# Encoder trunk in split float32r: sequence 1's last steps of the second MLP product, moved from the loop to behind it

## The chip, the cores and the metric

The kernel runs on one core of a Trainium2 chip. A core has five engines that run their own instruction streams in order and wait for each other on semaphores: TensorE (PE in the profile) multiplies matrices into PSUM, VectorE (DVE) and ScalarE (ACT) work elementwise on SBUF and PSUM, GpSimd (POOL) elementwise on SBUF, and SyncE (SP) issues most of the DMAs. The metric is the device time of one execution in microseconds. Before the change it is 1680.16 us, the median of three runs (1679.12 to 1681.12).

## The reference

Two sequences of 512 tokens with 1024 features go through two layers and a last norm. Layer 0 mixes tokens with a 2-D Fourier transform, layer 1 with grouped-query attention; each is followed by a squared-ReLU MLP.

```python
def sq_relu_mlp(h, w_up, w_down):
    a = jnp.maximum(h @ w_up, 0)
    return (a * a) @ w_down

for i in range(DEPTH):
    j = i // N_MIXERS
    if i % N_MIXERS == 0:
        x = x + fourier_mix(rms_norm(x, fourier_norm[j]), fourier_w_out[j])
    else:
        x = x + gqa_attention(rms_norm(x, attn_norm[j]), attn_w_qkv[j], attn_q_norm[j],
                              attn_k_norm[j], attn_w_o[j])
    x = x + sq_relu_mlp(rms_norm(x, mlp_norm[i]), mlp_w_up[i], mlp_w_down[i])
return rms_norm(x, final_norm)
```

## The kernel before, in words

**Number format.** All large products run in float32r, each operand split into a high and a low half, three matmuls for one product. A split is a ScalarE copy (L86) and a VectorE subtraction (L87). A split with a gain per feature is a ScalarE activation (L90) and a VectorE instruction (L91); `make_h` uses it for the operands of attention.

**The residual.** Both sequences' residual streams are held transposed, features on partitions: `xs[q, m]` with q = 0, 1 the sequence and m = 0 to 3 a quarter of the features, each tile 128 x 2 x 512. The half of a quarter is called `fo` = 2m or 2m + 1. `put_away` stores such a tile to DRAM (`park`) with a DMA on the SP queue. `square` has ScalarE square one half (L160); GpSimd adds the squares of all eight halves into one tile (L164), and `sums` has TensorE add that tile over the partitions (L172), which gives the sum of squares for each token. `token_scale` turns it into the scale of the RMS norm, in a chain of short VectorE and ScalarE instructions (L135 to L140).

**The MLP.** Both sequences together go through each layer's MLP as a 2 x 2 block product with seven products in place of eight (Winograd's form). The second product, `second_product`, loops over groups of the hidden features and over m. For each m it has two `Row` products and five `Sums` products, whose results VectorE adds from PSUM (L1113) to `xs[0, m]`, `xs[1, m]` or to `e[m]`, a tile that is part of several results. TensorE's order is as written; the other engines' order is set by a scheduler. The weights arrive by DMA (`w_row`, `w_sum`), are combined on VectorE (L1183, L1184, L1190) and split (L86, L87). When all products of an m are done, `finish(m)` adds `e[m]` to a half of `xs[0, m]` (L1253) and to both halves of `xs[1, m]` (L1254), and calls `ready(m)`.

**Between the layers.** In layer 0 `ready(m)` makes, for both sequences and both halves, the operand of attention (`make_h`) and the square, and stores the tile. Behind the loop come the tables for the rotary embedding (16 VectorE instructions, L1382, from a table `rope` and the gains `grow`, both loaded by DMA on SP), and then the products for queries, keys and values. `begun` starts the four token tiles of sequence 0's keys and values with six of eight feature chunks, 72 matmuls; the scale of sequence 0, the remaining 24 matmuls, the scale of sequence 1 and its four tiles of 24 matmuls each follow. VectorE, ScalarE and GpSimd normalize and rotate the keys tile by tile (L1440 is the last step of a tile), and TensorE transposes sequence 0's keys (L1451).

**After layer 1's loop** nothing is made ready: the last two pairs of hidden features, kept apart as plain weights (`w_down`), are projected one eighth of the features at a time, `project(0, fo)` for sequence 0 first (matmuls L81 to L83, the addition L891), each followed by a square and a gain for the output; sequence 1 follows.

Of the kernel before, what the change touches and what calls it, by code (L numbers as in the profile page):

```python
# [19 lines left out]
P = 128  # L20
D = 1024
S = 512
NSEQ = 2
NT = S // P
KC = D // P
# [19 lines left out]
def trunk_kernel(ctx, tc, x_in, xt_in, y_out, tables, rope, gfour, gcol, grow, gfin,  # L45
                 w_four, w_nyq, w_qkv, w_o, w_a22, w_up, w_row2, w_row4, w_sum2, w_sum4, w_down):
    nc = tc.nc
# [13 lines left out]
    def nm(s):  # L61
        n_[0] += 1
        return f"{s}_{n_[0]}"

    def slot(shape, dt):
        return act.tile(shape, dt, tag="u4", name=nm("u"))

    def tm(shape=(P, 512), dt=F32):
        return tmp.tile(list(shape), dt, tag="t2", name=nm("t"))
# [4 lines left out]
    def ps():  # L74
        return psp.tile([P, 512], F32, tag="ps", name=nm("ps"))
# [4 lines left out]
    def mm3(out, lh, ll, rh, rl, first, last):  # L80
        nc.tensor.matmul(out, lh, rh, start=first, stop=False)  # L81
        nc.tensor.matmul(out, lh, rl, start=False, stop=False)  # L82
        nc.tensor.matmul(out, ll, rh, start=False, stop=last)  # L83
# [5 lines left out]
    def split_scaled(dst_hi, dst_lo, src, scale):  # L89
        nc.scalar.activation(dst_hi, src, AF.Copy, scale=scale)  # L90
        nc.vector.scalar_tensor_tensor(dst_lo, src, scale, f32(dst_hi), ALU.mult, ALU.subtract)  # L91
# [34 lines left out]
    def rsqrt(out, ss, n, inv, room=None):  # L126
        for step in rsqrt_steps(out, ss, n, inv, room=room):
            step()
# [16 lines left out]
    xs, acc, apart = {}, {}, {}  # L145
# [6 lines left out]
    def xt(q, fo):  # L152
        return xs[q, fo // 2][:, fo % 2]

    def square(q, fo, n=512, alone=False, first=0):

        if fo == first:
            acc[q] = tm()
        s = acc[q] if fo == first else tm()
        nc.scalar.activation(s[:, :n], xt(q, fo)[:, :n], AF.Square)  # L160
        if alone:
            apart[q] = s
        elif fo != first:
            nc.gpsimd.tensor_add(acc[q][:, :n], acc[q][:, :n], s[:, :n])  # L164

    def sums(q, n=NT):

        o = ps()
        parts = [acc[q]] + ([apart.pop(q)] if q in apart else [])
        for t in range(n):  # L170
            for i, x in enumerate(parts):
                nc.tensor.matmul(o[:, 2 * t : 2 * t + 2], x[:, t * P : (t + 1) * P], ones,  # L172
                                 start=i == 0, stop=i == len(parts) - 1)
        return o[:, 0 : 2 * n : 2], o[:, 64:]
# [9 lines left out]
    def make_h(q, fo, g0):  # L184

        h = slot([P, 2, 512], F32R)
        split_scaled(h[:, 0], h[:, 1], xt(q, fo), gc[:, g0 + fo : g0 + fo + 1])
        return h
# [3 lines left out]
    def put_away(q, i):  # L192
        nc.sync.dma_start(park[q, i], xs[q, i])
# [475 lines left out]
    def even_outs(q, fos):  # L669
        return outs(q, fos, we, 0, 258, (wn.w, un[q]))  # L670
# [30 lines left out]
    ET = mybir.EngineType  # L701
    with tc.manual_schedule(engines={ET.PE, ET.Activation, ET.DVE, ET.Pool, ET.SP}):
# [128 lines left out]
        blocks = Blocks(0)  # L831
# [11 lines left out]
        for fo in range(KC):  # L843
            e, = even_outs(1, [fo])
# [14 lines left out]
        rows = []  # L859
# [234 lines left out]
    def second_product(l, blocks, rows, late=lambda: None, ready=lambda m: None):  # L1094
        e, new = [], [True] * 4
# [154 lines left out]
        def finish(m):  # L1250
            left[m] -= 1
            if left[m] == 0:
                nc.vector.tensor_add(xs[0, m][:, 1], xs[0, m][:, 1], e[m])  # L1253
                nc.vector.tensor_add(xs[1, m], xs[1, m], e[m].unsqueeze(1).broadcast_to([P, 2, 512]))  # L1254
                ready(m)

        first_product(l, blocks, rows, ahead)
# [16 lines left out]
        rows, sums = items[0]  # L1274
# [28 lines left out]
        for k, (rows, sums) in enumerate(items):  # L1303
# [40 lines left out]
            for r in rows:  # L1344
                finish(r.m)
            finish(sums.m)


    hT, rs, wkv = [[], []], [], []

    def token_scale(q):
        r = sm.tile([P, NT], F32, tag="rs", name=nm("rs"), bufs=2)
        ss, room = sums(q)
        rsqrt(r, ss, NT, 1.0 / D, room)
        rs.append(r)
# [4 lines left out]
        wkv.append(lent())  # L1360
        split(*wkv[-1], raw)

    def ready(m):
        for q in range(NSEQ):
            for fo in range(2 * m, 2 * m + 2):
                hT[q].append(make_h(q, fo, KC))
                square(q, fo)
            put_away(q, m)

    second_product(0, blocks, rows, late, ready)  # L1370

    gb = tm((P, 4, HD))
    nc.sync.dma_start(gb, grow.to_broadcast([P, 4, HD]))
# [12 lines left out]
    def qkv(cg, q, t, ws, k0=0, k1=KC, o=None):  # L1386
        o = ps() if o is None else o
        cols = slice(t * P, (t + 1) * P)
        for k in range(k0, k1):
            w = ws[k // 2]  # L1390
            c = (k % 2) * 512
            mm3(o, hT[q][k][:, 0, cols], hT[q][k][:, 1, cols],
                w[0][:, c : c + 512], w[1][:, c : c + 512], k == 0, k == KC - 1)
        return o
# [176 lines left out]
    transposes = {(0, 0, 0): 0, (0, 1, 0): 1}  # L1571

    begun = [qkv(2, 0, t, wkv, 0, KC - 2) for t in range(NT)]
    token_scale(0)
    keeping, turned = keep(), iter(())
    ws = {2: wkv}
# [104 lines left out]
    blocks = Blocks(2 * KC)  # L1681
    nc.scalar.activation(one[:, :1], last[:, :1], AF.Sqrt)

    todo, e, rows = heads_out.plain_sums(), [tm() for _ in range(4)], []
    load_xs(0, park[0])

    def add(x, o):
        nc.vector.tensor_add(x, o, x)
# [9 lines left out]
    with tc.manual_schedule(engines={ET.PE}):  # L1698
# [39 lines left out]
        for j, (m, i) in enumerate(turn()):  # L1738
# [3 lines left out]
            fo = 2 * m + 1 - i  # L1742
# [12 lines left out]
                blocks.first_lo(j - 3)  # L1755
        for i in range(2, 4):
            blocks.first_lo(i)
    second_product(1, blocks, rows)
    ats = []
    for f in range(2 * PLAIN):  # L1760
        raw = load_raw(plain[f], (P, 2, 512))
# [50 lines left out]
    def tokens(t):  # L1812

        x = slot([P, D], F32)
        for h in range(2):
            o = ps()
            for k in range(4):
                nc.tensor.transpose(o[:, k * P : (k + 1) * P], xt(1, 4 * h + k)[:, t * P : (t + 1) * P], ident)
            nc.scalar.copy(x[:, h * 512 : (h + 1) * 512], o)
        return x  # L1820

    with tc.manual_schedule(engines={ET.PE, ET.Activation, ET.DVE, ET.Pool, ET.SP}):
        oa, ob, oc, oe = OutT(0, 4), OutT(1, 2), Out(2), Out(3)
        for fo in range(KC):
            project(0, fo, ws, [a[0] for a in ats])
            square(0, fo)
            oa.gain(fo)
        xtok = [tokens(2), tokens(3)]
        for fo in range(KC):
            project(1, fo, ws, [a[1] for a in ats], 256)  # L1830
            square(1, fo, 256, fo == KC - 1)
            ob.gain(fo)
            if fo == 1:
                oa.root()
            if fo == 3:
                oa.spread()
            if fo > 3:
                oa.write(fo - 4)

        x, z = xtok  # L1840
        y = slot([P, D], F32), slot([P, D], F32)
        groups = ((0, 512), (512, 768), (768, 1024))

        def tile(t, c0, c1, at=0, mid=lambda: None):
            o = ps()[:, : c1 - c0]
            for k in range(len(ats)):
                ak, wk = ats[k][1], ws[k]
                cols = slice(t * P, (t + 1) * P)
                mm3(o, ak[0][:, cols], ak[1][:, cols], wk[0][:, c0:c1], wk[1][:, c0:c1], k == 0, k == len(ats) - 1)
                if k == at:  # L1850
                    mid()
            return o

        def add(x, o, c0, c1):
            nc.vector.tensor_add(x[:, c0:c1], o, x[:, c0:c1])

        def write(x, y, r, i):
            sl = slice(i * 512, i * 512 + 512)
            nc.vector.scalar_tensor_tensor(y[:, sl], x[:, sl], r, gf[:, sl], ALU.mult, ALU.mult)

        o = [tile(2, 0, 512, 2, ob.root)]
        add(x, o[0], 0, 512)
        o.append(tile(2, 512, 1024, 0, ob.spread))
        oc.square(x[:, :512], 0)
        ob.write(0)
        add(x, o[1], 512, 1024)
        oc.square(x[:, 512:], 1)
        o = [tile(3, 0, 512)]
        ob.write(1)
        ob.write(2)  # L1870
        root = oc.root(1)
        for step in root[:2]:
            step()
        ob.write(3)
        for step in root[2:]:
            step()
        add(z, o[0], *groups[0])
        oe.square(z[:, :512], 0)
        write(x, y[0], oc.r, 0)
        o += [tile(3, *g) for g in groups[1:]]  # L1880
        add(z, o[1], *groups[1])
        oe.square(z[:, 512:768], 1)
        write(x, y[0], oc.r, 1)
        nc.sync.dma_start(y_out[2][:P], y[0])
        root = oe.root(2)
        add(z, o[2], *groups[2])
        oe.square(z[:, 768:], 2)
        nc.vector.tensor_mul(y[1][:, 512:768], z[:, 512:768], gf[:, 512:768])
        root[0]()
        root[1]()  # L1890
        nc.vector.tensor_mul(y[1][:, 768:], z[:, 768:], gf[:, 768:])
        for step in root[2:]:
            step()
        nc.scalar.activation(y[1][:, 512:], y[1][:, 512:], AF.Copy, scale=oe.r)
        nc.scalar.dma_start(y_out[2][P:, 512:], y[1][:, 512:])
        write(z, y[1], oe.r, 0)
        nc.sync.dma_start(y_out[2][P:, :512], y[1][:, :512])
# [151 lines left out]
```

## Time and profile before

| | us |
|---|---|
| median of three runs | 1680.16 (1679.12 to 1681.12) |
| the profiled execution's own time | 1682.5 |
| its span, first to last instruction | 1680.5 |
| TensorE busy | 1666.0 |
| VectorE busy | 1258.9 |
| ScalarE busy | 873.4 |
| GpSimd busy | 394.5 |
| layer 0's second product ends, queries, keys and values begin | at 708.6 of the span |
| layer 1's second product ends, the last projections begin | at about 1624 of the span |

The mean granted TensorE clock is 0.998 of full speed.

How to read the rows: a row of the timeline has the start in microseconds, how long the group took, the engine, the line of the code, the operation, what is written and read, and in brackets the engine's idle time before it and who ended it. Equal instructions that follow each other are one row (xN). A row of the windows has the stretch, its length, then for TensorE, its weight loads, VectorE, ScalarE and GpSimd the busy time and the number of instructions, the granted clock, the DMA engines' busy share and GB/s. A row of the waits has who waited for whom, the sum in microseconds, how often, and the longest. A group's row has the count, the busy time, the mean in ns, and the idle time before it. Of a line or a tile, one row gives the shortest, median and longest duration in ns and the first and last start.

### The profile page before, as it was taken

What the parts mean: (1) busy time and instruction counts of PE and PEld (TensorE: products, weight loads), DVE (VectorE), ACT (ScalarE), POOL (GpSimd) and SP (SyncE); (2) the same over time, 40 slices, a digit from 0 to 9 for tenths busy, and PEclk for the clock granted to TensorE, in tenths of its full rate; (3) what the DMA queues carried; (4) which work ended last, traced back from release to release, by engine and by line L of the source; (5) the groups of instructions that cost most, each with busy time, mean ns of one, the idle gap of its engine ahead of it and who ended that gap; (6) DMA issues with size and microseconds to landing.
All of it is one profiled execution on the core that took longest, in us unless ns stands there. A gap on an engine that the chain in (4) does not pass through costs nothing.

```text
span 1680.5 us, 22279 instructions
## 1 busy us (share of the span) xinstructions
PE 1666.0 (99%) x7845; PEld 1387.7 (83%) x7845; DVE 1258.9 (75%) x1848; ACT 873.4 (52%) x1537; POOL 394.5 (23%) x364
## 2 busy tenths in 40 slices
PE   9999999999999999999999999999999999999998
PEld 8988888888888888788878888888888888888887
DVE  8879776557786779869888877777855487878865
ACT  6766444456343425447698854554544553433334
POOL 3321443221000001325544303004422220000002
PEclk9999999999999999999999999999999999999999
DMA  9843655459775757425501146334544696757532
GB/s 310 262 151 111 209 194 182 145 176 371 242 231 170 254 171 225 168 65 196 168 1 39 63 164 224 124 114 160 209 156 155 226 367 203 232 158 237 176 102 100
DMA packets 122047, 302.99 MB, mean 180 GB/s; under 512 B 12200, under 2 KB 13352, under 8 KB 121936
## 3 DMA queue, kind: packets, MB, share of 16 engines
q1 hardware_dynamic: 98576, 254.05, 43.6%
q0 software_dynamic: 8960, 21.05, 5.9%
q10 hardware_dynamic: 14400, 26.48, 4.2%
q8 instruction: 61, 1.00, 0.2%
q14 instruction: 50, 0.41, 0.1%
HBM read 218.11 MB, written 82.38 MB: 179 GB/s over the span
## 4 chain that ended last, share of the span: by engine, by line
PE 87%; DVE 6%; ACT 3%; issue 2%; DMA 2%; POOL 0%; SPq 0%; DVEq 0%; ACTq 0%; POOLq 0%
PE ps L907 69%; PE ps L83 5%; PE ps L81 5%; PE ps L82 5%; PE ps L1482 1%; DVE w L87 1%; ACT t L1474 1%; ACT u L86 1%; DVE u L87 1%; DVE u L219 1%; DVE u L235 1%; DVE u L1113 0%; DMA u<-w_four 0%; DMA u<-x 0%; PE ps L172 0%
## 5 line engine op out<-in xcount | busy, mean ns | idle before, releaser
L907 PE MATMUL ps<-u,w 128*128 128x512 f32 x4944 | 1133.3, 390 | 2.9 <-DVE w L87 2.1
L907 PEld LDWEIGHTS ps<-u,w 128*128 128x128 f32 x4944 | 927.5, 188 | 199.1 <-DVE w L87 3.2
L86 ACT CAST w<-raw 128x1024 fp32r<-128x1024 f32 (+1 forms) x216 | 214.0, 996 | 310.9 <-PE ps L907 229.0
L87 DVE TENSOR_TENSOR w<-raw,w 128x1024 fp32r<-128x1024 f32 (+1 forms) x216 | 252.3, 1172 | 77.6 <-ACT w L86 77.3
L86 ACT CAST u<-u 128x1024 fp32r<-128x1024 f32 x144 | 145.2, 1049 | 83.8 <-PE ps L907 36.5
L87 DVE TENSOR_TENSOR u<-u,u 128x1024 fp32r<-128x1024 f32 x144 | 173.3, 1230 | 19.0 <-ACT u L86 17.9
L907 PE MATMUL ps<-u,u 128*128 128x512 f32 x600 | 143.1, 389 | 0.1
L1142 POOL DMA_DIRECT2D raw<-w_sum x32 | 27.7, 866 | 469.3 <-DMA raw<-w_sum 197.9
L1113 DVE TENSOR_TENSOR u<-ps,u 128x512 f32<-128x512 f32 x160 | 109.6, 686 | 37.2 <-PE ps L907 34.4
L1023 POOL TENSOR_TENSOR u<-u 128x512 f32<-128x512 f32 x28 | 37.7, 1345 | 424.7 <-ACT u L920 424.7
L907 PEld LDWEIGHTS ps<-u,u 128*128 128x128 f32 x600 | 112.5, 188 | 23.8 <-ACT u L938 0.5
L81 PE MATMUL ps<-u,u 128*128 128x512 f32 (+2 forms) x340 | 128.8, 381 | 0.4 <-ACT t L1474 0.3
L82 PE MATMUL ps<-u,u 128*128 128x512 f32 (+2 forms) x340 | 124.2, 366 | 0.4 <-DVE u L87 0.3
L83 PE MATMUL ps<-u,u 128*128 128x512 f32 (+2 forms) x340 | 124.4, 366 | 0.1
L164 POOL TENSOR_TENSOR t<-t,t 128x512 f32<-128x512 f32 (+1 forms) x54 | 77.8, 1446 | 190.6 <-ACT t L160 189.9
L919 ACT ACTIVATE t<-t 128x512 f32<-128x512 f32 x64 | 40.5, 632 | 109.8 <-DVE t L992 99.8
L87 DVE TENSOR_TENSOR u<-ps,u 128x512 fp32r<-128x512 f32 (+3 forms) x112 | 68.5, 635 | 7.9 <-ACT u L86 7.3
L83 PEld LDWEIGHTS ps<-u,u 128*128 128x128 f32 x340 | 64.2, 189 | 10.5 <-DVE u L448 0.5
L81 PEld LDWEIGHTS ps<-u,u 128*128 128x128 f32 x340 | 64.3, 189 | 10.1 <-ACT u L86 1.5
L82 PEld LDWEIGHTS ps<-u,u 128*128 128x128 f32 x340 | 64.4, 189 | 9.2 <-DVE u L87 1.4
L979 DVE TENSOR_TENSOR t<-ps,u 128x512 f32<-128x512 f32 x32 | 22.0, 688 | 60.5 <-PE ps L907 52.7
L1476 POOL TENSOR_SCALAR t<-t,s 128x512 f32<-128x512 f32 x64 | 47.3, 740 | 74.0 <-DVE s L1475 60.1
(260 smaller groups left out, 2029.7 us busy)
## 6 DMA issues: line engine op xcount, KB each, us to landing
raw<-w_up SPq DMA_DIRECT2D x80, 512.0 KB, 4.6
u<-spill_t SPq DMA_DIRECT2D x60, 512.0 KB, 6.8
raw<-w_sum SPq DMA_DIRECT2D x56, 512.0 KB, 5.7
u<-spill_b SPq DMA_DIRECT2D x45, 512.0 KB, 6.2
spill_t<-u SPq DMA_DIRECT2D x84, 256.0 KB, 2.0
spill_b<-t ACTq DMA_DIRECT2D x60, 256.0 KB, 4.3
raw<-w_row SPq DMA_DIRECT2D x28, 512.0 KB, 5.2
park<-u SPq DMA_DIRECT2D x24, 512.0 KB, 4.5
```

What stands on the lines that cost most here:

```text
L81: nc.tensor.matmul(out, lh, rh, start=first, stop=False)
L82: nc.tensor.matmul(out, lh, rl, start=False, stop=False)
L83: nc.tensor.matmul(out, ll, rh, start=False, stop=last)
L86: nc.scalar.copy(dst_hi, src)
L87: eng.tensor_sub(dst_lo, src, f32(dst_hi))
L164: nc.gpsimd.tensor_add(acc[q][:, :n], acc[q][:, :n], s[:, :n])
L907: nc.tensor.matmul(o, w[x][:, sl], h[k][y], start=first and k + i == 0, stop=k == n - 1 and i == 2, skip_group_check=not first)
L919: nc.scalar.activation(t, src, AF.Relu)
L1023: eng.tensor_sub(t[:, 0], b12, b11)
L1113: nc.vector.tensor_add(x, o, x)
L1142: nc.gpsimd.dma_start(s[:, 1], w[:, 3], accum_op=ALU.add)
L1476: nc.gpsimd.tensor_scalar(p, p, sm_[:, :1], 1.0, ALU.mult, ALU.mult)
```

## The change

`finish` no longer adds `e[m]` to sequence 1 and makes only sequence 0 ready. `second_product` returns a function `other(m)` that does the addition to `xs[1, m]`. In layer 0 it is called behind the begun products, for m = 0 to 3, each time followed by sequence 1's squares, operands and store, with VectorE and ScalarE in the written order there. In layer 1 it is called in the loop of sequence 0's projection, for the first four `fo`. `ready` now does the square of a half ahead of its operand. No arithmetic is added or removed.

```diff
@@ second_product
             left[m] -= 1
             if left[m] == 0:
                 nc.vector.tensor_add(xs[0, m][:, 1], xs[0, m][:, 1], e[m])
-                nc.vector.tensor_add(xs[1, m], xs[1, m], e[m].unsqueeze(1).broadcast_to([P, 2, 512]))
                 ready(m)
...
             finish(sums.m)
 
+        def other(m):
+            nc.vector.tensor_add(xs[1, m], xs[1, m], e[m].unsqueeze(1).broadcast_to([P, 2, 512]))
+
+        return other
...
-    def ready(m):
-        for q in range(NSEQ):
-            for fo in range(2 * m, 2 * m + 2):
-                hT[q].append(make_h(q, fo, KC))
-                square(q, fo)
-            put_away(q, m)
-
-    second_product(0, blocks, rows, late, ready)
+    def ready(m, q=0):
+        for fo in range(2 * m, 2 * m + 2):
+            square(q, fo)
+            hT[q].append(make_h(q, fo, KC))
+        put_away(q, m)
+
+    other = second_product(0, blocks, rows, late, ready)
...
     begun = [qkv(2, 0, t, wkv, 0, KC - 2) for t in range(NT)]
+    with tc.manual_schedule(engines={ET.Activation, ET.DVE}):
+        for m in range(4):
+            other(m)
+            ready(m, 1)
     token_scale(0)
...
-    second_product(1, blocks, rows)
+    other = second_product(1, blocks, rows)
...
             project(0, fo, ws, [a[0] for a in ats])
             square(0, fo)
             oa.gain(fo)
+            if fo < 4:
+                other(fo)
```

## The prediction

> **What bounds the kernel now.** I read the page first, then TensorE's waits, then the timeline around the one wait that counts.
>
> ```profile
> span 1680.5 us, 22279 instructions
> PE 1666.0 (99%) x7845; PEld 1387.7 (83%) x7845; DVE 1258.9 (75%) x1848; ACT 873.4 (52%) x1537; POOL 394.5 (23%) x364
> PE ps L907 <- DVE w L87: 2.1, 2, 1.9
> PE ps L907 <- DVE u L1688: 0.7, 1, 0.7
> ```
>
> TensorE is busy 99% of the span, so moving VectorE (DVE), ScalarE (ACT) or GpSimd (POOL) work pays only where TensorE stops. In the products (L907) it stops for L87, the lower half of a weight split, twice, 2.1 us in all, 1.9 of it in one wait. The next rows place that wait and show the clock behind it.
>
> ```profile
> 660.62 12.63 PE L907 MATMUL ps<-u,w 128*128 128x512 f32 x55
> 696.46 12.34 PE L907 MATMUL ps<-u,w 128*128 128x512 f32 x46 [1.91 <-DVE w L87]
> 708.64 0.39 PE L81 MATMUL ps<-u,u 128*128 128x512 f32 x1
> ...
> 698.00:699.00 1.00, 1.00 (x3) 0.74 (x3) 1.00 (x2) 1.00 (x3) 0.40 (x1) 0.50 0.71 262
> 699.00:700.00 1.00, 1.00 (x4) 0.77 (x3) 0.00 (x0) 1.00 (x2) 1.00 (x2) 0.50 1.07 287
> 700.00:701.00 1.00, 1.00 (x4) 0.80 (x3) 0.69 (x1) 0.02 (x1) 1.00 (x1) 0.50 0.79 168
> 701.00:702.00 1.00, 1.00 (x5) 0.80 (x5) 0.00 (x0) 0.00 (x0) 0.92 (x2) 0.96 0.99 397
> ...
> 685.00:694.50 9.50, 9.50 (x43) 7.57 (x41) 9.47 (x10) 5.36 (x8) 7.69 (x4) 1.00 0.36 118
> ```
>
> The wait ends at 696.46, at the end of layer 0's second product. A full-clock matmul takes (12.63-0.39)/54 = 0.227 us. The 46 after the wait take 12.18 us until the next line starts at 708.64, against 46 x 0.227 = 10.43: 1.75 us more, and in those microseconds the granted clock is 0.50. So the wait costs 1.9 + 1.75 = 3.7 us. In the 9.5 us before it VectorE is busy for 9.47: its backlog is the cause.
>
> **The change, part by part: inside the loops.** By the built program's order, the addition L1254 of m = 1 and 2 and sequence 1's L91 of all m leave the crowded stretch (the addition of m = 0 is written behind the loop too, but the scheduler still places it inside). The rows price them.
>
> ```profile
> L1254 DVE TENSOR_TENSOR u<-u,t 128x1024 f32<-128x1024 f32 x3 | 3.7, 1222 | 0.0
> L91 DVE SCALAR_TENSOR_TENSOR u<-u,gc,u 128x512 fp32r<-128x512 f32 x12 | 11.3, 960 | 0.1
> ...
> 667.53 2.98 POOL L164 TENSOR_TENSOR t<-t,t 128x512 f32<-128x512 f32 x2 [0.62 <-ACT t L160]
> 667.98 1.38 DVE L91 SCALAR_TENSOR_TENSOR u<-u,gc,u 128x512 fp32r<-128x512 f32 x1
> 669.28 1.77 DVE L1184 TENSOR_TENSOR raw<-raw 128x512 f32<-128x512 f32 x1
> ```
>
> Five of them stood ahead of the split that TensorE waited for, two L1254 and three L91: 2 x 1.22 + 3 x 0.96 = 5.3 us of VectorE, and GpSimd's additions of sequence 1's squares go with them. The last three rows show what those do: a VectorE instruction with both operands in SBUF (L91, L1184) takes twice its time while GpSimd adds; the two take turns. 5.3 us is well over the wait of 1.9, so I expect it to vanish with the slow clock behind it: **-3.7 us**. Layer 1's loop gains nothing; TensorE has no wait there:
>
> ```profile
> 1410.00:1624.00 214.00, 214.00 (x945) 177.10 (x944) 172.65 (x226) 77.85 (x88) 10.38 (x12) 1.00 0.60 190
> ```
>
> **Behind layer 0's loop.** Here the moved work must be done again in time. What TensorE does there, and the prices:
>
> ```profile
> 724.96 0.95 PE L172 MATMUL ps<-ones,t 128*128 128x2 f32 x8
> ...
> 732.23 0.39 PE L81 MATMUL ps<-u,u 128*128 128x512 f32 x1
> ...
> 754.00 1.03 PE L1451 MATMUL ps<-ident,u 128*128 128x128 f32 x8
> ...
> 712.18 0.69 DVE L1253 TENSOR_TENSOR u<-u,t 128x512 f32<-128x512 f32 x1
> 714.86 3.04 DVE L91 SCALAR_TENSOR_TENSOR u<-u,gc,u 128x512 fp32r<-128x512 f32 x2 [0.38 <-ACT u L90]
> ...
> L1382 DVE SCALAR_TENSOR_TENSOR u<-raw,t x16: 277/278/1154, 718.0 to 722.0; 128x128 f32<-128x128 f32 x16
> ...
> 713.60 0.62 ACT L160 ACTIVATE t<-u 128x512 f32<-128x512 f32 x1
> 714.12 0.70 ACT L90 ACTIVATE u<-u,gc 128x512 fp32r<-128x512 f32 x1
> 714.74 0.62 ACT L160 ACTIVATE t<-u 128x512 f32<-128x512 f32 x1
> ...
> 714.36 4.70 POOL L164 TENSOR_TENSOR t<-t,t 128x512 f32<-128x512 f32 x3 [10.62 <-ACT t L160]
> ...
> 713.32 0.40 SPq L1373 DMA_DIRECT2D t<-grow  x1
> ...
> DMA to landing us min/median/max: 4.7/4.7/4.7
> ...
> DMA to landing us min/median/max: 2.6/4.5/10.9
> ```
>
> TensorE first, on before's clock less 3.7 us. The loop ends at 704.9. The 72 begun matmuls take 724.96-708.64 = 16.3, sequence 0's sums (L172) 0.8, the other 24 matmuls of sequence 0's four tiles 5.4. In the built program sequence 1's sums now stand behind those 24 (before, behind 6). TensorE comes to them at **727.5**, and they need all eight squares of sequence 1.
>
> Now VectorE, ScalarE, GpSimd and the SP queue, in the built order. Sequence 0's last addition ends about 0.9 after the loop, L1253 0.7 later, at 706.5. SP then issues its store and, as before, the gains (grow) 0.45 later (712.87 to 713.32), at 707.0: one store ahead of them now, two before. They land 4.7 us after issue by their own row, and not before the fastest store's 2.6; I take 3.9, as one store less stands ahead: 710.9. The sixteen table instructions (L1382) stand on VectorE **ahead** of sequence 1's operands and wait for that landing; they take 0.2 us each outside the first, 3.3 in all: 714.2. Then m = 0: L1254 was done in the loop, its two L91 take 1.3: 715.5. Then m = 1, 2, 3, written out as addition, square, operand, square, operand. One round: the addition 1.13; ScalarE's first square, up to GpSimd's start, 0.77; then GpSimd's addition and L91 take turns twice, 1.24 + 0.66 each (the 4.70 row is three such additions against L91): 1.13 + 0.77 + 3.8 = 5.7; I take 5.6. Without taking turns it is ScalarE's four steps (0.52 + 0.62 + 0.52 + 0.70, by the starts above) between an addition and an L91: 4.3. The three additions end at 716.7, 722.3 and 727.9. VectorE's first step of sequence 0's scale (L135) stands between the second one and its L91s and waits for TensorE's sums at 722.0: no delay. After the third addition come two squares and two GpSimd additions, 3.9 with turns and 3.4 without: **731.8**. TensorE waits 731.8 - 727.5 = **4.3 us**. Bounds: no turns, 716.7 + 8.6 + 3.4 = 728.7, so 1.2; gains landing only after 4.7, so 5.1. I take 4.3 because the turns have rows in this very place.
>
> A wait that long is followed by the slow clock, as the 1.9 us wait was: 3.4 us at 0.50, **+1.7 us** (the 0.7 us wait at L1688 has no half-clock row: the window behind it grants 1.00).
>
> ```profile
> 1048.00:1049.00 1.00, 1.00 (x6) 0.82 (x5) 1.00 (x2) 0.63 (x2) 0.93 (x1) 1.00 0.00 0
> ```
>
> The Trainium skill, TensorE: Matmul & The Clock Gate, section "Part 1: The HAM clock gate", has the clock halved after at least one idle window of about 3.4 us. This trace had it after 1.9, so the measurement decides; with a wait of 4.3 us both give +1.7, and a wait of 2 to 3 us would be free of it by the page alone, which would take 1.7 off the sum.
>
> If the clock stays up, something else costs about as much. The normalization of sequence 0's keys starts after both sums; TensorE transposes the keys (L1451) behind 96 matmuls.
>
> ```profile
> 729.03 0.46 ACT L90 ACTIVATE u<-ps,rs 128x256 fp32r<-128x256 f32 x1
> 749.51 1.66 POOL L1440 TENSOR_TENSOR u<-t,t 128x256 f32<-128x256 f32 x1 [3.20 <-DVE t L1438]
> ```
>
> First L90 to last key addition: 751.17 - 729.03 = 22.1. After: sums end 732.6, L90 one later, keys at 755.7. TensorE arrives at 732.6 + 96 x 0.227 = 754.4, or 756.1 with the slow clock. So either 1.7 of slow clock, or 1.3 of waiting for keys. Before, the gap there was 754.00 - 751.17 = 2.8 of slack.
>
> **Behind layer 1's loop.** The four additions go between the projections' own. They are hidden (2.06 us of idle VectorE in front of each L891). The last w_down split (L87) now stands behind L1253 and not ahead of it; TensorE was already on it.
>
> ```profile
> 1625.34 1.22 DVE L87 TENSOR_TENSOR w<-raw,w 128x1024 fp32r<-128x1024 f32 x1
> 1626.48 0.68 DVE L1253 TENSOR_TENSOR u<-u,t 128x512 f32<-128x512 f32 x1
> 1629.90 0.69 DVE L891 TENSOR_TENSOR u<-ps,u 128x512 f32<-128x512 f32 x1 [2.06 <-PE ps L83]
> ...
> 1626.62 0.50 PE L83 MATMUL ps<-u,w 128*128 128x512 f32 x1
> ```
>
> L1253 holds VectorE 0.67; some 0.3 of that comes back, since nothing is ahead of the tile's addition any more: **+0.3 us** (0 to 0.7).
>
> **Sum.** -3.7 + 4.3 + 1.7 + 0.3 = **+2.6 us**: 1683.1 for the profiled span of 1680.5, 1685.1 for that execution's own 1682.5. The median of the runs, 1680.16, stands 2.3 below that execution; I add the 2.6 to it: **1682.8 us**.
>
> **The rivals.**
> *The moved work is covered (not slower).* VectorE and GpSimd don't collide, the wait at the sums is the lower bound 1.2, too short for the slow clock, and keys are late by about the 1.3 worked out above at most, say 0.5: -3.7 + 1.2 + 0.5 + 0.3 = -1.7, 1678.5. For it: GpSimd rests 10.62 us before its three additions at 714.36. Against it: the squares and L91 come in pairs by the written order, so each addition meets an L91. Chance 0.13.
> *The slow clock lasts two windows (slower).* The place is TensorE's restart at sequence 1's sums; the price is a second 3.4 us at 0.50, 1.7 more; it decides if the wait is so long that the clock falls during it and the first window after it doesn't count as busy. -3.7 + 4.3 + 3.4 + 0.3 = +4.3, 1684.5; with the gains landing after 4.7, 1685.3. For it: a wait twice that of before. Against it: before shows one window only. Chance 0.25.
> *The change doesn't do what it says.* The loop's wait stays, because the split waits for its weights' landing or ScalarE and not for VectorE's backlog: +2.6 + 3.7 = +6.3, 1686.5. For it: VectorE still carries sequence 0's work there. Against it: 9.47 of 9.50 busy. Chance 0.05.
>
> **How the numbers follow.** The forecast has 0.53, its own range 1681.0 to 1684.4. The remaining 0.04 is unnamed. Within 0.2% of 1680.16, 3.4 us, is about what a measurement of this kernel can tell from no change, so 1676.8 to 1683.5. Of the forecast 0.38 lies within and 0.15 above; of the covered case 0.12 within and 0.01 faster; the two windows and the failed change are above; of the rest 0.02 is faster and 0.02 within. Faster 0.03, same 0.52, slower 0.45. The range, from the covered case's neighbourhood to the failed change's: 1679.0 to 1686.3.
>
> **What would show it.** Loop: no TensorE wait and no 0.50 clock near 690 to 702. Tail: a TensorE wait at L172 some 22 us after the loop, released by GpSimd's L164, of 3.5 to 5 us, with 0.50 behind it; pairs of L164 and lengthened L91 in front of it; the table instructions waiting for grow. Layer 1: a few tenths at the first projection. Wrong would be a wait at the sums under 2 us, one at the key transposes of more than 1.5, or a wait left in the loop.

## The result, and the profile after

| | us |
|---|---|
| before, median of six runs | 1679.64 (1678.57 to 1684.17) |
| after, median of six runs | 1687.42 (1685.51 to 1691.89) |
| ratio after to before | 1.0045 (95% interval 1.0031 to 1.0059) |
| the profiled execution after, its span | 1688.0, 1686.2 |

The kernel became slower by 0.45%, some 7.6 us. The prediction had 1682.8 with a range up to 1686.3: the right sign, and a loss far too small.

The page of the kernel after and TensorE's waits on it (who waited for whom, the sum, how often, the longest):

```profile
span 1686.2 us, 22297 instructions
PE 1667.2 (99%) x7845; PEld 1388.7 (82%) x7845; DVE 1260.5 (75%) x1848; ACT 872.7 (52%) x1537; POOL 391.7 (23%) x364
PE ps L172 <- POOL t L164: 4.2, 1, 4.2
PE ps L907 <- DVE t L1113: 1.5, 1, 1.5
PE ps L907 <- DVE u L1113: 0.8, 1, 0.8
```

The wait of 1.9 us for L87 is gone (0.2 us is left of it), and a new wait of 4.2 us at sequence 1's sums (L172) stands at the top: both as forecast. Two more are new, 0.8 us in layer 0's loop at 686 and 1.5 us in layer 1's loop at 1557. The timeline of the kernel after behind layer 0's loop shows how the 4.2 us come about:

```profile
705.20 0.39 PE L81 MATMUL ps<-u,u 128*128 128x512 f32 x1
707.27 0.38 SPq L1376 DMA_DIRECT2D t<-grow  x1
711.23 3.32 DVE L1385 SCALAR_TENSOR_TENSOR u<-raw,t 128x128 f32<-128x128 f32 x16 [1.69 <-DMA t<-grow]
715.80 1.22 DVE L1348 TENSOR_TENSOR u<-u,t 128x1024 f32<-128x1024 f32 x1
717.88 2.98 POOL L164 TENSOR_TENSOR t<-t,t 128x512 f32<-128x512 f32 x2 [6.70 <-ACT t L160]
718.39 3.03 DVE L91 SCALAR_TENSOR_TENSOR u<-u,gc,u 128x512 fp32r<-128x512 f32 x2 [1.37 <-ACT u L90]
721.34 1.21 DVE L1348 TENSOR_TENSOR u<-u,t 128x1024 f32<-128x1024 f32 x1
726.88 1.22 DVE L1348 TENSOR_TENSOR u<-u,t 128x1024 f32<-128x1024 f32 x1
729.24 2.94 POOL L164 TENSOR_TENSOR t<-t,t 128x512 f32<-128x512 f32 x2 [2.83 <-ACT t L160]
732.24 1.87 PE L172 MATMUL ps<-ones,t 128*128 128x2 f32 x8 [4.16 <-POOL t L164]
734.94 0.46 ACT L90 ACTIVATE u<-ps,rs 128x256 fp32r<-128x256 f32 x1
755.38 2.25 POOL L1443 TENSOR_TENSOR u<-t,t 128x256 f32<-128x256 f32 x1 [3.20 <-DVE t L1441]
757.77 1.03 PE L1454 MATMUL ps<-ident,u 128*128 128x128 f32 x8
```

(L1348, L1376, L1385, L1443 and L1454 are the lines L1254, L1373, L1382, L1440 and L1451 of before, moved by the edit.) The gains (grow) arrive, the tables are built, and only then three rounds follow, 5.54 us each from one L1348 to the next. In a round two L91 on VectorE take 3.0 us, and two L164 on GpSimd, in much the same stretch, 3.0 as well. The last key is ready at 755.38 + 2.25 = 757.63, and TensorE comes to the key transposes 0.14 later: if the keys can't be ready sooner, TensorE could not have gone on much earlier there even with no wait at the sums. The sums later, below, put that to the test.

The windows of the kernel after around the end of that wait (TensorE's busy time, its weight loads, VectorE, ScalarE, GpSimd, then the granted clock):

```profile
731.00:732.00 1.00, 0.00 (x0) 0.00 (x0) 1.00 (x2) 0.00 (x0) 1.00 (x1) 0.61 0.01 4
732.00:733.00 1.00, 0.76 (x4) 0.76 (x4) 0.81 (x2) 0.00 (x0) 0.18 (x1) 0.50 0.00 0
737.00:738.00 1.00, 1.00 (x4) 0.71 (x4) 0.75 (x5) 0.44 (x2) 0.00 (x0) 0.50 0.00 0
738.00:739.00 1.00, 1.00 (x6) 0.81 (x5) 0.51 (x2) 0.45 (x3) 0.00 (x0) 0.98 0.00 0
```

A mean of 0.61 over a microsecond means 0.78 of it at 0.50, so the half clock lasts from 731.22 to 738.04: 6.8 us, twice the 3.4 us of before.

Three times of each trace divide the span where the change acts: the first matmul behind layer 0's loop (the first L81 there), the first key transpose, and the end. The stretch between the first two I call the tail.

| us | loop ends | tail | rest | span |
|---|---|---|---|---|
| before | 708.64 | 45.36 | 926.50 | 1680.5 |
| after | 705.20 | 52.57 | 928.43 | 1686.2 |
| difference | -3.44 | +7.21 | +1.93 | +5.7 |

The 7.21 are 4.16 of waiting and 3.05 of slower matmuls. The 1.93 contain the 1.5 us wait in layer 1's loop.

### The profile page after: what moved, and what is told of

It reads as the page before. It is cut to its first block, busy times and chain, and to the rows that moved or that the text cites. A ratio compares the mean times of both kernels' runs of the same rounds, so it can differ in the third digit from the quotient of the medians.

```text
span 1686.2 us, 22297 instructions
## 1 busy us (share of the span) xinstructions
PE 1667.2 (99%) x7845; PEld 1388.7 (82%) x7845; DVE 1260.5 (75%) x1848; ACT 872.7 (52%) x1537; POOL 391.7 (23%) x364
## 4 chain that ended last, share of the span: by engine, by line
PE 86%; DVE 6%; ACT 3%; DMA 3%; issue 1%; POOL 0%; SPq 0%; DVEq 0%; ACTq 0%; POOLq 0%
PE ps L907 68%; PE ps L83 5%; PE ps L81 5%; PE ps L82 5%; DMA raw<-w_sum 1%; PE ps L1485 1%; ACT u L86 1%; DMA u<-w_qkv 1%; ACT t L1477 1%; DVE w L87 1%; DVE u L87 1%; DVE u L1113 1%; DVE u L219 1%; DVE u L91 1%; DVE u L235 1%
## 5 line engine op out<-in xcount | busy, mean ns | idle before, releaser
L87 DVE TENSOR_TENSOR w<-raw,w 128x1024 fp32r<-128x1024 f32 (+1 forms) x216 | 250.5, 1164 | 80.6 <-ACT w L86 80.4
L87 DVE TENSOR_TENSOR u<-u,u 128x1024 fp32r<-128x1024 f32 x144 | 173.0, 1228 | 18.2 <-ACT u L86 17.4
L1113 DVE TENSOR_TENSOR u<-ps,u 128x512 f32<-128x512 f32 x160 | 109.5, 685 | 42.4 <-PE ps L907 39.8
L81 PE MATMUL ps<-u,u 128*128 128x512 f32 (+2 forms) x340 | 129.6, 384 | 0.5 <-ACT t L1477 0.3
L164 POOL TENSOR_TENSOR t<-t,t 128x512 f32<-128x512 f32 (+1 forms) x54 | 76.9, 1424 | 204.7 <-ACT t L160 203.8
L160 ACT ACTIVATE t<-u 128x512 f32<-128x512 f32 (+1 forms) x64 | 38.4, 603 | 70.4 <-DVE u L1695 22.8
L87 DVE TENSOR_TENSOR u<-ps,u 128x512 fp32r<-128x512 f32 (+3 forms) x112 | 68.4, 634 | 7.9 <-ACT u L86 7.4
L81 PEld LDWEIGHTS ps<-u,u 128*128 128x128 f32 x340 | 64.9, 191 | 10.3 <-ACT u L86 1.5
```

Source lines behind the costliest of these rows:

```text
L87: eng.tensor_sub(dst_lo, src, f32(dst_hi))
```

## The experiments

The theory at the start, called "the tail" in the expectations, was that the wait at the sums and the half clock behind it are the loss. The rivals were layer 1's wait, the length of the moved additions themselves, and later VectorE's late end.

**The changed kernel once more** (no edit).

> The changed kernel once more, for what comes back from execution to execution. Theory (the tail): ratio 1.0045 within 0.0015; TensorE waits 4.2 us within 0.3 for GpSimd's L164 at sequence 1's sums (L172), with 6.8 us at clock 0.50 behind it; the wait of 0.8 us in layer 0's loop comes back, because it follows from the written order of square and operand. Rival (layer 1): the wait of 1.5 us in layer 1's loop, at 1555 of the span, belongs to the change and comes back with 1.5 within 0.3. If it is the landing of one accumulated w_sum transfer, which came 5.9 us after its issue and 5.0 in the kernel before, it is under 0.5 or gone.

Measured: ratio 1.0037 (1.0024 to 1.0050), span 1686.9. The waits of this execution:

```profile
PE ps L172 <- POOL t L164: 4.8, 1, 4.8
PE ps L473 <- ACT t L409: 2.0, 1, 2.0
PE ps L907 <- DVE u L1113: 0.5, 1, 0.5
```

The tail's wait comes back, somewhat longer than the bound of 0.3 allowed, the loop's small wait too, and layer 1's wait is gone: it is not a fixed part of the change. The half clock is longer still, by its windows:

```profile
731.00:732.00 1.00, 0.00 (x0) 0.00 (x0) 0.74 (x1) 1.00 (x3) 1.00 (x1) 0.66 0.73 295
741.00:742.00 1.00, 1.00 (x4) 0.77 (x4) 0.40 (x4) 0.92 (x4) 0.00 (x0) 0.72 0.00 0
```

By the same arithmetic it lasts from 731.32 to 741.56, 10.2 us.

**Layer 0's half alone, and layer 1's half alone.**

```diff
 # layer 0's half alone: layer 1's additions stay in finish
                 nc.vector.tensor_add(xs[0, m][:, 1], xs[0, m][:, 1], e[m])
+                if l == 1:
+                    nc.vector.tensor_add(xs[1, m], xs[1, m], e[m].unsqueeze(1).broadcast_to([P, 2, 512]))
...
-            if fo < 4:
-                other(fo)
```

> Only layer 0's half of the change; layer 1's four additions stand inside its loop as before. Theory (the tail): layer 1's half costs 0.2 us, so this is within 0.5 us of the changed kernel: ratio to before 1.0044. Rival (layer 1): without its half the 1.5 us wait at 1555 and the 0.2 at the projections are gone, 1.7 us under the changed kernel: ratio 1.0035.

In the other kernel `if l == 1` is `if l == 0`, `ready` is that of before, and the block behind `begun` is left out.

> Only layer 1's half of the change; layer 0 is as before. Theory (the tail): 0.2 us over before, ratio 1.0001, TensorE's wait of 1.9 us for L87 near 695 and 3.4 us at 0.50 behind it are there as before, and no wait at 1555. Rival (layer 1): 1.7 us over before, ratio 1.0010, with a wait of 1.5 us for L1113 at 1555.

Measured: layer 0's half 1.0036 (1.0026 to 1.0046), layer 1's half 0.9993 (0.9984 to 1.0003). Layer 0's half alone doesn't tell the two expectations apart, for 1.0044 and 1.0035 both lie in its interval; layer 1's half alone rules the rival's 1.0010 out, and it has no wait at 1555. The loss is layer 0's. Layer 1's half costs nothing that can be told; the 0.3 us of the prediction is smaller than these runs tell apart. With layer 0's half alone, where layer 1's loop is as before, TensorE waited 1.5 us in all for the same line L1113 in layer 1's loop, 1.1 of it in one wait at 1558, so that wait does not come from layer 1's edit either. The kernel with layer 1's half alone has layer 0 as before, and its waits on TensorE for L87 (sum, how often, the longest) are not those of before, though they were expected to be, with the half clock behind them:

```profile
PE ps L907 <- DVE w L87: 0.6, 2, 0.4
```

**The kernel before once more** (no edit), because of that row.

> The kernel before once more, one look. Theory (the wait of 1.9 us for L87 in layer 0's loop and the window at 0.50 behind it belong to one execution: the kernel with only layer 1's half, whose layer 0 is as before, had 0.4 and 0.2 there and no such window): wait at L87 under 1.5 us, no window at 0.50 near 695, span 1677 to 1679. Rival (they come each time): 1.9 us and 3.4 us at 0.50, span 1680 to 1681.

Measured: span 1681.1, and in its timeline on TensorE

```profile
696.35 10.72 PE L907 MATMUL ps<-u,w 128*128 128x512 f32 x46 [1.28 <-DVE w L87]
```

The wait is there with 1.28 us, and the 46 matmuls take 10.72 us, not 12.34: no half clock behind it. The span is above what either theory expected. This execution also had three waits for L1113 in layer 1's loop, 1.4 us in all, so the kernel before has such waits too; the rest of the excess is not traced. Of the three executions traced, the 3.7 us that the prediction took are the largest case. The loop ends at 708.64, 706.91 and 705.81 in the three traces whose layer 0 is as before, and at 705.20, 706.11 and 705.41 in the changed kernel, the same once more and layer 0's half alone: means of 707.12 and 705.57, a gain of 1.55. The tail in the same six is 45.36 each time before, and 52.57, 54.09 and 53.06 after: +7.88 in the mean.

**The tables behind the moved work.**

```diff
-    gb = tm((P, 4, HD))
-    nc.sync.dma_start(gb, grow.to_broadcast([P, 4, HD]))
...
     begun = [qkv(2, 0, t, wkv, 0, KC - 2) for t in range(NT)]
     with tc.manual_schedule(engines={ET.Activation, ET.DVE}):
         for m in range(4):
             other(m)
             ready(m, 1)
+    gb = tm((P, 4, HD))
+    nc.sync.dma_start(gb, grow.to_broadcast([P, 4, HD]))
...
```

> The changed kernel, but the sixteen table instructions (L1385) and the loads of grow and rope stand behind sequence 1's additions, squares, operands and stores. In the changed kernel VectorE waits 1.69 us for grow and then does 3.32 us of tables, and its first addition (L1348) starts at 715.80; here it can start some 4.9 us sooner. Theory (the tail): the wait at sequence 1's sums falls from 4.2 to under 0.5, no window at 0.50 stands behind it, and the time falls by 4.2 + 3.4 = 7.6 us to about the time before, ratio 1.0000 within 0.001; later waits at the key transposes (L1454) under 1 us, since the tables are needed only there. Rival (the additions themselves are too long, tables or not): the wait stays over 2 us, and the ratio is 1.003 or more.

Measured: ratio 1.0029 (1.0018 to 1.0040); the tail is 757.08 - 704.77 = 52.31. Its timeline, on VectorE, the SP queue and TensorE:

```profile
711.38 1.21 DVE L1348 TENSOR_TENSOR u<-u,t 128x1024 f32<-128x1024 f32 x1
716.92 1.21 DVE L1348 TENSOR_TENSOR u<-u,t 128x1024 f32<-128x1024 f32 x1
724.06 0.42 SPq L1569 DMA_DIRECT2D t<-grow  x1
727.52 1.87 PE L172 MATMUL ps<-ones,t 128*128 128x2 f32 x8 [3.74 <-POOL t L164]
730.04 3.31 DVE L1578 SCALAR_TENSOR_TENSOR u<-raw,t 128x128 f32<-128x128 f32 x16
```

The first addition does start 4.4 us sooner and the squares are ready 4.7 sooner (0.4 of both from the loop's end), as the theory had it, and the wait is still 3.7 us, with 6.8 us of half clock from 726.90 to 733.72. The theory's expectation failed, and the rival's, a wait over 2 us, was met. Two things were not foreseen. The sums stand 17 matmuls further ahead on TensorE, so that it comes to them at 723.8: behind the loop TensorE's order, too, is the scheduler's, for the code calls the sums behind the 6 matmuls that finish sequence 0's first tile, and they stand behind 6 in the kernel before, 24 in the changed one and 7 here. And the tables now stand between the sums and the keys on VectorE, 3.3 us of it. The run says that the tables delay the moved work, and not yet which delay counts.

**The sums later.** This separates the wait at the sums (theory A) from VectorE's late end (theory B).

```diff
-        if (cg, q, t) == (2, 0, 0):
+        if (cg, q, t) == (2, 1, 0):
             token_scale(1)
```

> The changed kernel, but sequence 1's sums and scale stand behind the first tile of sequence 1 on TensorE, 24 matmuls or 5.4 us later, and the normalization of sequence 0's keys no longer stands behind them on VectorE. Theory A (the wait at the sums is the loss): additions ready at 732, TensorE there at 733: no wait at L172, no window at 0.50, the time 7.3 us under the changed kernel, ratio 1.000 within 0.001. Theory B (VectorE's late end of sequence 1's operands is the loss, and the sums only show it first): VectorE is free for the keys at 732.7 as before, the keys need 22 us from there (22.1 in the kernel before), so they end at 755; TensorE reaches the key transposes (L1454) at 722.3 + 0.8 + 120 x 0.227 = 750.3, waits 4.5 to 5 us there and has half clock behind it: 0 to 2 us under the changed kernel, ratio 1.003 to 1.004.

Measured: ratio 1.0048 (1.0036 to 1.0060), no wait at the sums, and in the timeline and the windows

```profile
734.06 0.47 ACT L90 ACTIVATE u<-ps,rs 128x256 fp32r<-128x256 f32 x1 [2.25 <-DVE rs L140]
756.37 1.64 POOL L1443 TENSOR_TENSOR u<-t,t 128x256 f32<-128x256 f32 x1 [5.06 <-DVE t L1441]
758.06 0.69 PE L1454 MATMUL ps<-ident,u 128*128 128x128 f32 x2 [4.80 <-POOL u L1443]
757.00:758.00 1.00, 0.00 (x0) 0.00 (x0) 1.00 (x2) 0.00 (x0) 1.00 (x1) 0.70 0.00 0
760.00:761.00 1.00, 1.00 (x5) 0.76 (x4) 0.17 (x1) 1.00 (x7) 0.00 (x0) 0.60 0.08 29
```

Theory B's wait of 4.5 to 5 us is there with 4.80, and half clock from 757.40 to 760.80, and theory A is out; the loss is as large as the changed kernel's, where B had up to 2 us less. The wait at the sums is only the first place where VectorE's lateness shows. VectorE gets to the end of sequence 0's scale only behind sequence 1's operands, at 733.6 here, and the keys took 24.0 us from their first step (734.06) to their last (758.01), against 22.1 before.

**The wait filled.**

```diff
+                idle = ps()
+                for k in range(18):
+                    nc.tensor.matmul(idle, hT[0][0][:, 0, 0:P], ws[2][0][0][:, 0:512], start=k == 0, stop=k == 17)
                 token_scale(1)
```

The last products of sequence 0's four tiles are called together ahead of it.

> The changed kernel with 18 needless matmuls of 0.227 us each on TensorE between the 24 matmuls and sequence 1's sums, into a PSUM tile that nobody reads: the 4.2 us of waiting are filled, so that the clock should not fall, while VectorE, ScalarE and GpSimd do the same as in the changed kernel. Theory (the keys' chain is the bound, the half clock stands in its cover): no window at 0.50; sums end near 733.0, one later the first key operand, 22.7 us later (734.94 to 757.63 in the changed kernel) the last key: 756.6; TensorE reaches the key transposes (L1454) at 733.0 + 96 x 0.227 = 754.8 and waits some 1.8 us there: about 1.2 us under the changed kernel. Rival (the half clock is a loss of its own, 3.1 us in the changed kernel: half of the 6.2 us in which TensorE works at 0.50): no wait at L1454 and 3.1 us under the changed kernel.

Measured: ratio 1.0037 (1.0024 to 1.0049). The timeline of this kernel on TensorE:

```profile
728.16 4.24 PE L1611 MATMUL ps<-u,u 128*128 128x512 f32 x18
732.60 1.05 PE L172 MATMUL ps<-ones,t 128*128 128x2 f32 x8 [0.20 <-POOL t L164]
757.27 0.76 PE L1454 MATMUL ps<-ident,u 128*128 128x128 f32 x5 [1.41 <-POOL u L1443]
```

And a window of it, where the changed kernel has 0.50:

```profile
735.00:738.00 3.00, 3.00 (x15) 2.49 (x14) 1.82 (x8) 1.47 (x6) 0.00 (x0) 1.00 0.00 0
```

The clock stays at 1.00, and the keys are waited for by 1.4 us. From the loop's end to the last transpose it is 757.27 + 0.76 - 705.44 = 52.6 us, against 757.77 + 1.03 - 705.20 = 53.6 in the changed kernel: 1.0 us less where 1.2 was expected and the rival had 3.1. The medians can't tell 1 us apart, and each row is one execution: once more and layer 0's half alone had 55.1 and 54.1 for the same stretch, 2.5 and 1.5 more than the filled kernel. The half clock cost 3.1, 4.0 and 3.2 us in these three (the tail beyond 45.36, less the wait). So between a third and two thirds of it lie in the cover of the keys: the theory fits the changed kernel's own trace, and the longer half clock of another execution is in part a loss of its own.

**GpSimd's additions left out.**

```diff
-        elif fo != first:
+        elif fo != first and not apart_only:
             nc.gpsimd.tensor_add(acc[q][:, :n], acc[q][:, :n], s[:, :n])
...
-            square(q, fo)
+            square(q, fo, apart_only=q == 1)
```

> The changed kernel without GpSimd's seven additions (L164) of sequence 1's squares: the squares are made and not added, the scale of sequence 1 is that of its first half quarter alone, and sequence 1's sums stand behind all of sequence 0's tiles. Asked is the length of a round behind the loop, from one addition L1348 to the next, 5.54 us in the changed kernel, in which two L91 take 3.03 us. Theory (L91 and L164 take turns): L91 alone takes 0.75 as in the rows without GpSimd, the pair 1.4 to 1.6, and a round is ScalarE's four steps and no more: 4.3 us; sequence 1's operands end 2 x 1.24 + 1.5 = 4 us sooner than 732.7, and the wait at the key transposes, where there is one, is under 1.5 us; ratio 1.000 to 1.001. Rival (L91 is slow there for another reason): the round stays 5.5 us, and the keys are waited for by 4 to 5 us; ratio 1.004.

The sums are called three tiles later, where they stood in the changed kernel as built. Measured: ratio 1.0014 (1.0004 to 1.0023). The timeline of this kernel on VectorE and TensorE:

```profile
717.47 1.23 DVE L1348 TENSOR_TENSOR u<-u,t 128x1024 f32<-128x1024 f32 x1
720.07 0.75 DVE L91 SCALAR_TENSOR_TENSOR u<-u,gc,u 128x512 fp32r<-128x512 f32 x1 [1.37 <-ACT u L90]
721.20 0.75 DVE L91 SCALAR_TENSOR_TENSOR u<-u,gc,u 128x512 fp32r<-128x512 f32 x1 [0.38 <-ACT u L90]
721.87 1.22 DVE L1348 TENSOR_TENSOR u<-u,t 128x1024 f32<-128x1024 f32 x1
755.40 0.44 PE L1454 MATMUL ps<-ident,u 128*128 128x128 f32 x2 [2.89 <-POOL u L1443]
1555.64 4.60 PE L907 MATMUL ps<-u,w 128*128 128x512 f32 x12 [2.13 <-DVE t L1113]
```

An L91 takes 0.75 us again and a round 4.40, where the prediction's case without turns had 4.3: GpSimd's additions beside them are what makes a round 5.54. The wait for the keys was 2.9 us and not under 1.5, for the first addition stands at 717.47 here, behind grow and the tables, and the keys' chain took 24 us. The wait at 1555 is layer 1's again, the longest seen, with 3.4 us of half clock behind it.

**Another order behind the loop.** Additions first, then all squares, then all operands, then the tables.

```diff
         for m in range(4):
             other(m)
-            ready(m, 1)
+        for fo in range(8):
+            square(1, fo)
+        for m in range(4):
+            for fo in range(2 * m, 2 * m + 2):
+                hT[1].append(make_h(1, fo, KC))
+            put_away(1, m)
+    gb = tm((P, 4, HD))
...
```

> The changed kernel with another order behind the loop: all four additions of sequence 1, then its eight squares, then its eight operands with their stores, then the table instructions (L1385, there L1583) with their loads. In the built order the scheduler now places the additions in the loop as soon as their quarter is done; the operands L91 of sequence 1 stay behind the loop, ahead of the tables. Theory (the loss is the late end of sequence 1's squares and operands, 25 us behind the loop, from rounds in which each addition stands behind the operands of the quarter before, and from the tables ahead of them): squares end under 8 us and operands under 12 us behind the loop, TensorE waits neither at the sums, nor at the operands, nor at the key transposes, no window at 0.50, no wait over 1 us in the loop; 7 to 10 us under the changed kernel, ratio to before 0.998 to 1.000. Rival (VectorE has this work to do somewhere, and moving it can't gain): a wait of 2 us or more comes back in the loop at L87 or at the key transposes, ratio 1.001 or more.

Measured: ratio 1.0001 (0.9993 to 1.0010), span 1680.3. The timeline of this kernel at the end of the loop and behind it:

```profile
704.66 1.23 DVE L1348 TENSOR_TENSOR u<-u,t 128x1024 f32<-128x1024 f32 x1
710.54 10.96 POOL L164 TENSOR_TENSOR t<-t,t 128x512 f32<-128x512 f32 x7 [0.30 <-ACT t L160]
714.23 9.81 DVE L91 SCALAR_TENSOR_TENSOR u<-u,gc,u 128x512 fp32r<-128x512 f32 x8 [3.44 <-ACT u L90]
723.97 3.31 DVE L1583 SCALAR_TENSOR_TENSOR u<-raw,t 128x128 f32<-128x128 f32 x16
751.82 1.03 PE L1441 MATMUL ps<-ident,u 128*128 128x128 f32 x8
```

The tail is 751.82 - 706.46 = 45.36, that of before to the hundredth: no wait at the sums, the operands or the transposes. Squares and operands end later than expected (15 and 18 us behind the loop, not 8 and 12), and still in time. So the loss came from how the work stood behind the loop, and some 7 us of it go away here. But the run changes three things at once. The scheduler put all four additions back into the loop (the row of L1348 is the last; the others start at 658.1, 687.2 and 691.9), where the changed kernel had three of them, 3.7 us of VectorE, behind it; the squares stand ahead of all operands; and the tables stand last. With the tables moved alone, 3.7 us of waiting stayed; the shares of the other two were not separated. The loop ends at 706.46, with a wait of 0.75 for L1113 at 687: less than half of the mean gain of 1.55 against 707.12 is left, though one trace can't settle that.

**The same with sequence 0's operand ahead of its square**, as before.

> The order of squares_first with one more step: sequence 0's operand stands ahead of its square again, as in the kernel before. squares_first had a wait of 0.75 us for L1113 at 687, where GpSimd's L164 and VectorE's L91 run beside each other; the kernel before had none there. Theory (the pairing by the new order costs that): the wait at 687 is gone, 0.7 us under squares_first, ratio to before 0.9990 to 1.0000. Rival (it comes and goes from execution to execution, as the changed kernel's 0.84, 0.5 and, with layer 0's half alone, none): same as squares_first, ratio 1.000.

Measured: 1.0001 (0.9992 to 1.0010), span 1679.8, loop end 706.17, tail 45.36. The wait at 687 is gone, and the median is not lower: 0.7 us is less than these runs tell apart.

**Quarters 2 and 3 alone.**

```diff
+                if l == 0 and m < 2:
+                    nc.vector.tensor_add(xs[1, m], xs[1, m], e[m].unsqueeze(1).broadcast_to([P, 2, 512]))
                 ready(m)
+                if l == 0 and m < 2:
+                    ready(m, 1)
...
-        for m in range(4):
+        for m in range(2, 4):
             other(m)
             ready(m, 1)
```

The sums are called three tiles later.

> Layer 0's part for quarters 2 and 3 only; additions, operands and squares of quarters 0 and 1 of sequence 1 are called in the loop as before. The sums stand behind the 24 matmuls, as in the changed kernel. Behind the loop are one and a half rounds of 5.5 us in place of three. Theory: squares end near 722, no wait at the sums (TensorE there at 727.5); the keys' chain starts at 728.3 + 1 and ends near 751.5, TensorE reaches the transposes at 750.1: a wait of up to 1.5 us there, no half clock; the loop's wait at L87 between 0 and 1.9. Ratio 0.999 to 1.001. Rival (any part moved costs): ratio 1.002 or more, with a wait over 2 us behind the loop.

Measured: 1.0002 (0.9993 to 1.0011), span 1677.7, loop end 705.34, tail 45.43, a wait of 0.35 at L87 and none behind the loop. It has the loop's gain and not the tail's loss in its trace, and is no faster in its median: the 1 to 2 us that remain to be gained are as large as what comes and goes elsewhere. No version here is measurably faster than the kernel before.

## Why the prediction was wrong, point by point

- **Loop, -3.7.** The mechanism was right, the size wrong, and this is the first mis-sized term. The wait and its half clock were read from one execution, whose own time stood 2.3 us above the median, and then taken off the median. Over three executions with layer 0 as before the loop loses 3.7, some 1.5 and some 0.6, and the relief is 1.55 in the mean: 2.15 us of the prediction's error. A small wait for L1113 of up to 0.84 us at 686 was not foreseen; an L91 lengthened to 1.78 us beside L164 stands ahead of it, but the same L91 in layer 0's half alone brought no wait, so its cause stays open.
- **The wait at the sums, +4.3.** Right in place, releaser and size: 4.16 from 728.1 of the trace, 4.5 in the mean of three. The parts agree too: grow landed 3.9 us after its issue, the tables ended at 714.5 (714.2 predicted), the additions L1348 ended at 717.0, 722.6 and 728.1 (716.7, 722.3, 727.9), the squares at 732.2 (731.8). The landing, chosen between two bounds, was in part luck: the change once more waited 2.31 us for grow on VectorE, not 1.69, and its wait at the sums was 4.76. That the L164 beside it are what lengthens an L91 and the round was shown by leaving them out.
- **The half clock, +1.7.** This step failed: "3.4 us at 0.50" became 6.8 to 10.2 us. The tail's +7.88 less the 4.5 of waiting leaves 3.4, twice the term and 1.7 us of the error. The rival of two windows had the length of three of the four traces with a wait at the sums, and its condition, that the first window behind the wait doesn't count as busy, fits the rows. It had a chance of 0.25 and would have been the better forecast, though its 1684.5 was still 2.9 us short, in the main for the same -3.7 in the loop.
- **The keys, in place of the half clock.** The prediction's "either, or" was right, and it deserved more weight: without the half clock TensorE waits for the keys, 1.4 us with the wait filled and 4.8 with the sums moved away. With the wait filled and the clock at 1.00, the stretch from the loop's end to the last transpose is 52.6 us against 754.00 + 1.03 - 708.64 = 46.4 before: 6.2 more, next to the 6.0 (4.3 + 1.7) that the prediction had for wait and half clock together. The keys' start was reckoned from sums at full clock; they took 1.87 us at 0.50 and not 0.95.
- **Layer 1, +0.3.** Not told apart from nothing. The 1.5 us wait of the profiled execution comes and goes.
- **The sum.** Predicted -3.7 + 4.3 + 1.7 + 0.3 = 2.6; measured -1.55 + 4.5 + 3.4 + 0.57 (the rest of the span, where the two means differ by less than single executions do) = 6.9, against 6.2 to 7.8 by the runs. The range was too narrow as well: its upper end, 1686.3, lay under the 1686.5 of its own last rival, and it added no rival to another, though a loop that gains little and two windows could come together, as they did.

## What to carry to other kernels

A wait that one profile shows is one draw: before its removal is taken off a median, look at a second execution, or let its share be the distance that this execution has from the median. Where an engine's backlog is moved, follow it to every consumer behind it on the same engine, not only to the first wait: here the wait at the sums and the wait for the keys were two faces of VectorE being some 5 us late, and taking away the first let the next show. What repaired it was another order of the moved work, which also let the scheduler put its additions back into the loop; the whole change then gained nothing that could be measured.

## What the runs showed of the hardware

The half clock at these waits came in multiples of 3.41 us, and its length did not follow from the wait's length: 3.4 us with waits of 1.9 (before), 2.1 (the additions left out, layer 1's loop) and 4.8 (the sums later), 6.8 with 3.7 (the tables behind), 4.2 and 4.5 (layer 0's half alone), 10.2 with 4.8 (the change once more), none with 1.3 (before once more) and 2.9 (the additions left out, the keys). The long ones all come with a wait at L172, where the first work is eight matmuls of 128 x 2, 1.87 us long; behind the other waits come large matmuls at once or, in the sums later, after two transposes of 0.69 us together. One reading that fits is that a stretch of 3.41 us has to be mostly filled with larger matmuls for the clock to return, and that these stretches start independently of the wait, which would explain 6.8 against 10.2. It is not shown, and the margin is narrow: in the sums later a stretch with 0.66 us of idle TensorE was enough (757.40 to the end of the wait at 758.06), in the change once more the second stretch, with 0.9 us of the small matmuls, was not. No run varied the first matmuls alone.

The Trainium skill, TensorE: Matmul & The Clock Gate, section "Part 1: The HAM clock gate", has a free-running window of 3413 ns and the full clock after one busy window, which agrees with these multiples.

Two VectorE instructions (L91) of 0.75 us each and two GpSimd additions (L164) of 1.3 us each take 3.0 us on each engine when they run side by side, 3.54 from the first start to the last end (717.88 to 721.42 in the changed kernel); one after the other they would be 4.1, side by side without hindrance 2.6. The 0.75 each returns when the additions are left out. The Trainium skill, SBUF — State Buffer, section "SBUF: two separate sides", has a port pair that either engine holds for a whole instruction where VectorE has two SBUF inputs; the trace agrees in the main, with the L91 of 0.75 alone and 3.03 / 2 us beside the additions.
